# Mixture-of-experts layer: gate and up weights in chunks of 512 columns, gates and ups in turn, and weights kept stationary in all wide visits

## The chip, the cores and the metric

One core of one Trainium2 chip runs the whole layer. The metric is device time in microseconds, smaller is better. TensorE is called PE here (PEld is its weight load), VectorE is DVE, ScalarE is ACT, GpSimd is POOL, SyncE is SP.

## The reference, cut to what matters

The layer has two parts: attention over 1024 tokens of width 1024, and a mixture of 32 experts of which each token takes four. The change touches the experts alone:

```python
def expert_block(args):                  # a block of tokens and its expert
    xb, e = args
    gu = xb @ w_gate_up[e] + b_gate_up[e]          # 1024 -> 2048: 1024 gates, then 1024 ups
    gate = jnp.minimum(gu[:, :D_FF], SWIGLU_LIMIT)
    up = jnp.clip(gu[:, D_FF:], -SWIGLU_LIMIT, SWIGLU_LIMIT)
    glu = gate * jax.nn.sigmoid(SWIGLU_ALPHA * gate)
    return ((up + 1.0) * glu) @ w_down[e] + b_down[e]
```

All is float32. Each expert has 8 MB of gate and up weights and 4 MB of down weights, 403 MB for the 32.

## The kernel before, in words

Up to about 660 us the kernel does attention, its projections and the routing; then come the experts, then a final norm.

**Visits.** The experts are sorted by load and planned with fixed capacities (`PLAN`, 568 tokens down to 32). A visit is one expert with up to 512 tokens in blocks of up to 128; there are 33. Visits 0 to 10 have more than one block and form the stream "H"; visits 11 to 32 have one block and form the stream "L". Visits 7 to 10 hold 248, 208, 176 and 144 tokens, each in two blocks (128 and 120, 80, 48, 16). Visits 19 to 32 have at most 64 tokens and are called plain: their weights are used as they were loaded, in plain float32.

**Steps.** A visit has 16 gate-and-up steps, one for each of four column chunks `c` and four pairs of contraction rows `kh`, and 8 steps for the down weights. A step uses 256 x 512 weights. Two steps share one load of 1 MB (`weights`, L1170): for gates and ups this is two DMAs of 512 KB, 256 columns of gates and the 256 columns of ups that go with them, for down weights one DMA of 512 columns. In visits that aren't plain each step's weights are split in a high and a low part in fp32r (`cook`, L1296: ACT makes the high part, DVE and POOL together the low part, L1304), and a product is three matmuls: high by high, high by low, low by high.

**Two forms of matmul.** In the row form (L1526 to L1552) a block's tokens are the stationary operand and 512 columns of weights stream past: six matmuls of 512 columns a step for a block of over 64 tokens, four for one of at most 64 (its high and low parts sit side by side). The result has tokens on partitions, `glu` (L1434) works on it, and the product has to be turned on PE (`settle`, `turn`, L1365) before the down weights can use it. In the wide form (L1507 to L1525) 128 x 128 of the weights are stationary and all tokens of the visit stream past: 24 matmuls of `span` columns a step, into four PSUM banks, one for each 128 columns of gates or ups. The result stands with gate columns on partitions, `glu_w` (L1412) works on it, and nothing has to be turned. `span` (L74) is the number of tokens where that is at least 256, else 0 (row form): visits 0 to 6 use the wide form, visits 7 to 10 and all of L the row form. Down weights always use the row form.

**Order.** `merged` (L96) interleaves the steps of H and L so that loads and PE time stay in balance, by a cost for each step (`pe_cost`, L89) and one for what is loaded. The first 32 steps are of H alone. `places` (L126) gives every load and every split one of ten buffers and a time; a load is issued on SP's queue when the buffer's last reader is done. Each wide step costs 0.01 us a token in the planner's eyes, a row step 1.30 us for a full block.

Of the kernel before, what the change touches and what calls it, by code (L numbers as in the profile page):

```python
# [30 lines left out]
KP = 2  # L31
# [42 lines left out]
def span(v):  # L74

    n = sum(b[1] for b in v[2])
    return n if n >= 256 else 0
# [143 lines left out]
class Kernel:  # L221
# [948 lines left out]
    def weights(self, t, e, kind, c, kh):  # L1170

        nc = self.nc
        rows = slice(128 * KP * kh, 128 * KP * kh + 512)
        if kind == "g":
            for u in range(2):
                c0 = 1024 * u + 256 * c
                w = nc.sync.dma_start(t[:, :, 256 * u:256 * u + 256],
                                      self.w_gate_up[0][bass.ds(e, 1), rows, c0:c0 + 256]
                                      .rearrange("a (k p) n -> p (a k) n", p=128))
        else:  # L1180
            w = nc.sync.dma_start(t, self.w_down[0][bass.ds(e, 1), rows, 512 * c:512 * c + 512]
                                  .rearrange("a (k p) n -> p (a k) n", p=128))
        self.loaded = w.ins
# [60 lines left out]
    def experts(self):  # L1244
# [13 lines left out]
        xs, hs, accs = {}, {}, {}  # L1258
# [59 lines left out]
        def get_bias(n):  # L1318
# [14 lines left out]
            nt = max(nt for _, nt in vis[n][2])  # L1333
            o = groups(vis[n], nt)[-1]
            if st == "H":
                o, nt = 0, 128
# [75 lines left out]
        def glu_w(n, f, j, pg, pu):  # L1412

            sp = span(vis[n])
            if f == j == 0:
                hs[n] = parts("h", n)
            kk = 2 * f + j
            bc = biases[n]
            g = wp.tile([128, 512], F32, name="t", bufs=3)[:, :sp]
            a = wp.tile([128, 512], F32, name="sg", bufs=2)[:, :sp]  # L1420
            u = wp.tile([128, 512], F32, name="t", bufs=3)[:, :sp]
            V.tensor_scalar(g, pg[:, :sp], bc[:, kk:kk + 1], LIM, op0=ALU.add, op1=ALU.min)
            A.activation(a, g, AF.Sigmoid, scale=ALPHA)
            V.tensor_scalar(u, pu[:, :sp], bc[:, 8 + kk:9 + kk], LIM + 1.0, op0=ALU.add, op1=ALU.min)
            V.tensor_tensor(a, a, g, op=ALU.mult)
            V.scalar_tensor_tensor(a, u, 1.0 - LIM, a, op0=ALU.max, op1=ALU.mult)
# [7 lines left out]
        def glu(b, p, f):  # L1434
            nt = b["nt"]
            if len(late) == 4:
                settle(*late[0][1:3])
            t = wp.tile([128, 512], F32, name="t", bufs=3)[:nt]
            a = wp.tile([128, 256], F32, name="a", bufs=4)[:nt]
            bv = biases[b["n"]].rearrange("p (u n) -> p u n", u=2)[:, :, 256 * f:256 * f + 256]  # L1440
            t2 = t.rearrange("p (u n) -> p u n", u=2)
            *more, o = groups(vis[b["n"]], nt)
            V.tensor_tensor(t2, p[o:o + nt].rearrange("p (u n) -> p u n", u=2), bv[o:o + nt], op=ALU.add)
            for o in more:
                V.tensor_tensor(t, p[o:o + nt], t, op=ALU.add)
            V.tensor_scalar(t[:, 0:256], t[:, 0:256], LIM, None, op0=ALU.min)  # L1446
            V.tensor_scalar(t[:, 256:512], t[:, 256:512], LIM, -LIM, op0=ALU.min, op1=ALU.max)
            A.activation(a, t[:, 0:256], AF.Sigmoid, scale=ALPHA)  # L1448
            V.tensor_tensor(a, a, t[:, 0:256], op=ALU.mult)
            V.scalar_tensor_tensor(a, t[:, 256:512], 1.0, a, op0=ALU.add, op1=ALU.mult)  # L1450
            if f == b["j"] == 0:
                hs[b["n"]] = parts("h", b["n"])

            late.append((self.pe_time + 5.0, b, f, a))

        def settle(b=None, f=-1):

            for x in list(late):
                if x[0] <= self.pe_time or (x[1] is b and x[2] <= f):
                    late.remove(x)  # L1460
                    turn(x[3], hs[x[1]["n"]][1][x[1]["j"]][1:], x[1]["nt"], 2 * x[2])
# [32 lines left out]
        def mm(m):  # L1494
# [12 lines left out]
            if kind == "g" and span(vis[n]):  # L1507
# [4 lines left out]
                for j in range(2):  # L1512
                    for u in range(2):
                        ws = slice(256 * u + 128 * j, 256 * u + 128 * j + 128)
                        p = accs[n][2 * j + u][:, :sp]
                        for k in range(KP):
                            kk = KP * kh + k
                            mm(p, hi[:, k, ws], x[:, 0, kk, :], start=kk == 0, stop=False)  # L1518
                            mm(p, hi[:, k, ws], x[:, 1, kk, :], start=False, stop=False)  # L1519
                            mm(p, lo[:, k, ws], x[:, 0, kk, :], start=False, stop=kk == 7)  # L1520
                    if kh == NP - 1:
                        glu_w(n, c, j, accs[n][2 * j], accs[n][2 * j + 1])
# [3 lines left out]
            for b in blk[n]:  # L1526
                nt = b["nt"]
                if kind == "d":
                    settle(b, (KP * kh + KP - 1) // 2)
# [198 lines left out]
```

## Time and profile before

| | before |
|---|---|
| time, median of 3 runs | 2312.3 us (2306.0 to 2319.1) |
| the profiled execution | 2309.99 us, its span 2308.2 us |
| PE busy | 2110.6 us, 91% of the span |
| PE weight loads busy | 1516.9 us, 66% |
| DVE / ACT / POOL busy | 1635.7 / 964.0 / 1122.2 us |
| chain that ended last | PE 62%, DMA 14%, DVE 10%, issue 5%, POOL 4% |
| gate and up weights | 528 DMAs of 512 KB |
| down weights | 132 DMAs of 1024 KB |
| mean granted clock of TensorE | 0.97 |

Busy time of PE counts matmuls that overlap only once, so the page shows whether PE had something in flight, not how fast it went. How fast it goes is read from the starts of successive matmuls in the timeline. The chain is followed back from the last instruction; what it passes through is what the end waited for.

### The profile page before, as it was taken

What the parts mean: (1) busy time and instruction counts of PE and PEld (TensorE: products, weight loads), DVE (VectorE), ACT (ScalarE), POOL (GpSimd) and SP (SyncE); (2) the same over time, 40 slices, a digit from 0 to 9 for tenths busy, and PEclk for the clock granted to TensorE, in tenths of its full rate; (3) what the DMA queues carried; (4) which work ended last, traced back from release to release, by engine and by line L of the source; (5) the groups of instructions that cost most, each with busy time, mean ns of one, the idle gap of its engine ahead of it and who ended that gap; (6) DMA issues with size and microseconds to landing.
All of it is one profiled execution on the core that took longest, in us unless ns stands there. A gap on an engine that the chain in (4) does not pass through costs nothing.

```text
span 2308.2 us, 35345 instructions
## 1 busy us (share of the span) xinstructions
PE 2110.6 (91%) x11662; PEld 1516.9 (66%) x11662; DVE 1635.7 (71%) x3048; ACT 964.0 (42%) x1648; POOL 1122.2 (49%) x972
## 2 busy tenths in 40 slices
PE   4799998999878989889889999999999999999992
PEld 4787777777677877666555556655777686556551
DVE  7577645876576689789886545464777887767984
ACT  5343335763353455555553221122333343334443
POOL 1522222533565566897784233233455455455543
PEclk9899999999988999999999999999999999999996
DMA  7755486833567799999889999989998999899894
GB/s 250 181 156 160 140 224 170 193 78 131 133 173 191 231 284 296 290 275 295 257 278 338 351 290 337 335 298 318 286 294 269 312 310 321 281 309 299 300 315 158
DMA packets 468089, 583.40 MB, mean 253 GB/s; under 512 B 44245, under 2 KB 352645, under 8 KB 466057
## 3 DMA queue, kind: packets, MB, share of 16 engines
q1 hardware_dynamic: 444497, 528.41, 70.1%
q0 software_dynamic: 23408, 52.71, 11.2%
q8 instruction: 94, 1.54, 0.3%
q14 instruction: 90, 0.74, 0.1%
HBM read 522.41 MB, written 58.92 MB: 252 GB/s over the span
## 4 chain that ended last, share of the span: by engine, by line
PE 62%; DMA 14%; DVE 10%; issue 5%; POOL 4%; ACT 2%; SPq 1%; DVEq 0%; POOLq 0%; ACTq 0%
PE accL L1543 11%; DMA w<-in_w_gate_up 7%; PE accH L230 5%; PE accH L232 5%; PE accH L231 5%; PE accH L1518 4%; PE accH L1519 4%; PE accH L1520 4%; DVE w L1304 4%; POOL w L1304 3%; PE pm L230 3%; PE pm L232 3%; PE pm L231 2%; PE pt L1365 2%; PE poB L904 2%
## 5 line engine op out<-in xcount | busy, mean ns | idle before, releaser
L1304 POOL TENSOR_TENSOR w<-w,w 128x288 fp32r<-128x288 f32 x456 | 607.9, 1368 | 517.7 <-ACT w L1302 472.4
L1302 ACT ACTIVATE w<-w 128x1024 fp32r<-128x1024 f32 x456 | 469.6, 1053 | 502.7 <-DMA w<-in_w_gate_up 121.8
L1304 DVE TENSOR_TENSOR w<-w,w 128x736 fp32r<-128x736 f32 x456 | 499.0, 1103 | 183.4 <-ACT w L1302 172.2
L1518 PE MATMUL accH<-xH,w 128*128 128x256 f32 (+5 forms) x896 | 287.2, 323 | 3.3 <-ACT w L1302 1.5
L1519 PE MATMUL accH<-xH,w 128*128 128x256 f32 (+5 forms) x896 | 283.1, 316 | 0.4 <-DVE xH L238 0.4
L1520 PE MATMUL accH<-xH,w 128*128 128x256 f32 (+5 forms) x896 | 274.6, 317 | 0.6 <-POOL w L1304 0.5
L1518 PEld LDWEIGHTS accH<-xH,w 128*128 128x128 f32 x896 | 170.5, 191 | 47.6 <-issue 23.8
L1543 PE MATMUL accL<-w,xL 128*32 128x512 f32 (+3 forms) x896 | 181.3, 601 | 1.4 <-DVE y L1476 0.7
L1520 PEld LDWEIGHTS accH<-xH,w 128*128 128x128 f32 x896 | 171.1, 191 | 8.8 <-POOL w L1304 2.2
L1519 PEld LDWEIGHTS accH<-xH,w 128*128 128x128 f32 x896 | 171.2, 191 | 7.1 <-issue 1.6
L230 PE MATMUL accH<-w,hH 128*128 128x512 f32 (+3 forms) x368 | 151.4, 413 | 1.6 <-ACT w L1302 1.6
L231 PE MATMUL accH<-w,hH 128*128 128x512 f32 (+3 forms) x368 | 147.0, 399 | 0.0
L232 PE MATMUL accH<-w,hH 128*128 128x512 f32 (+3 forms) x368 | 144.7, 401 | 1.7 <-POOL w L1304 1.6
L1448 ACT ACTIVATE a<-t 32x256 f32<-32x256 f32 (+10 forms) x120 | 49.1, 412 | 175.7 <-DVE t L1446 175.2
L230 PE MATMUL accL<-w,xL 128*72 128x512 f32 (+4 forms) x256 | 104.7, 409 | 18.5 <-DVE y L1472 18.5
L232 PE MATMUL accL<-w,xL 128*72 128x512 f32 (+4 forms) x256 | 105.0, 411 | 14.7 <-POOL w L1304 13.9
L1478 POOL DMA_INDIRECT d_y<-y,lsH x54 | 88.6, 1640 | 46.5 <-DVE y L1472 33.5
L231 PE MATMUL accL<-w,xL 128*72 128x512 f32 (+4 forms) x256 | 103.9, 406 | 0.0
L1477 POOL TENSOR_TENSOR y<-y,gf 32x512 f32<-32x512 f32 (+6 forms) x40 | 63.9, 1598 | 70.7 <-DVE y L1476 70.6
L230 PEld LDWEIGHTS accH<-w,hH 128*128 128x128 f32 (+3 forms) x368 | 68.2, 186 | 45.8 <-issue 18.3
L230 PE MATMUL pm<-whi,hh 128*128 128x256 f32 x320 | 93.6, 293 | 2.1 <-ACT qs L538 1.0
L232 PE MATMUL pm<-wlo,hh 128*128 128x256 f32 x320 | 92.9, 291 | 0.0
(375 smaller groups left out, 4806.7 us busy)
## 6 DMA issues: line engine op xcount, KB each, us to landing
w<-in_w_gate_up SPq DMA_DIRECT2D x528, 512.0 KB
w<-in_w_down SPq DMA_DIRECT2D x132, 1024.0 KB
aw<-in_w_ada SPq DMA_DIRECT2D x64, 256.0 KB
wraw<-in_w_in SPq DMA_DIRECT2D x18, 512.0 KB
xt<-in_x SPq DMA_DIRECT2D x16, 512.0 KB
wa<-in_w_ada SPq DMA_DIRECT2D x8, 1024.0 KB
d_h<-zero SPq DMA_DIRECT2D x9, 512.0 KB
d_y<-zero SPq DMA_DIRECT2D x18, 256.0 KB
```

The lines of the kernel that those rows point to most:

```text
L230: mm(ps, lh, rh, start=start, stop=False)
L231: mm(ps, ll, rh, start=False, stop=False)
L232: return mm(ps, lh, rl, start=False, stop=stop).ins
L1302: A.activation(hi, w, AF.Copy)
L1304: eng.tensor_tensor(lo[:, :, cs], w[:, :, cs], hi[:, :, cs].bitcast(F32), op=ALU.subtract)
L1448: A.activation(a, t[:, 0:256], AF.Sigmoid, scale=ALPHA)
L1477: P.tensor_tensor(y, y, gf, op=ALU.mult)
L1478: s = P.indirect_dma_start(out=self.d_y[c], out_offset=bass.IndirectOffsetOnAxis(ap=b["ls"][:nt, 0:1], axis=0), in_=y, in_offset=None, com ...
L1518: mm(p, hi[:, k, ws], x[:, 0, kk, :], start=kk == 0, stop=False)
L1519: mm(p, hi[:, k, ws], x[:, 1, kk, :], start=False, stop=False)
L1520: mm(p, lo[:, k, ws], x[:, 0, kk, :], start=False, stop=kk == 7)
L1543: mm(p[o:o + nt], w[:, kk, :], hi[:, k, :], start=kk < len(at), stop=kk >= 8 - len(at))
```

## The change

Gate and up weights are loaded 512 columns at a time by one DMA of 1 MB: chunk 0 is the first half of the gates, chunk 1 the first half of the ups, then the second halves. Every visit with more than one block (0 to 10) uses the wide form for gates and ups. With at most 208 tokens (visits 8 to 10, "joined") the high and the low part of the tokens stream past the high weights in one matmul of twice the columns; the two halves of the sum are added behind it, with one more pass of ACT and one of DVE. A gate chunk leaves its activated gates in SBUF (`ga`, five buffers, or `a`, three) until the ups come. In the row form up to two pending products, of 512 columns each, wait to be turned, before it was four of 256. The planner's costs follow: 12 x KP x span / 2245 for a wide step, a formula of its own for joined visits. `mm` takes four groups of 128 columns of one kind in place of two groups of gates and ups:

```diff
 def span(v):
-    n = sum(b[1] for b in v[2])
-    return n if n >= 256 else 0
+    return sum(b[1] for b in v[2]) if len(v[2]) > 1 else 0
+def joined(v):
+    return 0 < span(v) <= 208
 def pe_cost(v, kind):
+    if kind == "g" and joined(v):
+        return 4 * KP * (2 * span(v) / 2245 + max(span(v) / 2245, 0.11))
     if kind == "g" and span(v):
-        return 12 * KP * span(v) / 2400
+        return 12 * KP * span(v) / 2245
...
         if kind == "g":
-            for u in range(2):
-                c0 = 1024 * u + 256 * c
-                w = nc.sync.dma_start(t[:, :, 256 * u:256 * u + 256],
-                                      self.w_gate_up[0][bass.ds(e, 1), rows, c0:c0 + 256]
-                                      .rearrange("a (k p) n -> p (a k) n", p=128))
+            c0 = 1024 * (c % 2) + 512 * (c // 2)
+            w = nc.sync.dma_start(t, self.w_gate_up[0][bass.ds(e, 1), rows, c0:c0 + 512]
+                                  .rearrange("a (k p) n -> p (a k) n", p=128))
...
+        def glu_w(n, c, j, p):
...
+            if joined(vis[n]):
+                A.activation(t, p[:, sp:2 * sp], AF.Copy)
+                V.scalar_tensor_tensor(t, p[:, :sp], bc, t, op0=ALU.add, op1=ALU.add)
+                V.tensor_scalar(t, t, top, None, op0=ALU.min)
+            else:
+                V.tensor_scalar(t, p[:, :sp], bc, top, op0=ALU.add, op1=ALU.min)
+            if c % 2 == 0:
+                a = gates[n, j] = wp.tile([128, WIDE], F32, name="ga", bufs=5)[:, :sp]
+                A.activation(a, t, AF.Sigmoid, scale=ALPHA)
+                V.tensor_tensor(a, a, t, op=ALU.mult)
+                return
...
+                for j in range(4):
+                    ws = slice(128 * j, 128 * j + 128)
+                    p = accs[n][j]
+                    for k in range(KP):
+                        kk = KP * kh + k
+                        if joined(vis[n]):
+                            mm(p[:, :2 * sp], hi[:, k, ws], x[:, :, kk, :], start=kk == 0, stop=False)
+                        else:
+                            mm(p[:, :sp], hi[:, k, ws], x[:, 0, kk, :], start=kk == 0, stop=False)
+                            mm(p[:, :sp], hi[:, k, ws], x[:, 1, kk, :], start=False, stop=False)
+                        mm(p[:, :sp], lo[:, k, ws], x[:, 0, kk, :], start=False, stop=kk == 7)
                     if kh == NP - 1:
-                        glu_w(n, c, j, accs[n][2 * j], accs[n][2 * j + 1])
+                        glu_w(n, c, j, p)
```

The row form's `glu` is divided in the same manner: each chunk adds the bias to 512 columns; a gate chunk then limits, activates and multiplies, an up chunk limits and multiplies into the kept gates.

## Rows read from the trace of the kernel before

**Rows 1.** Windows view, four stages of the experts; the header names the columns.

```profile
core 0: us, PE busy (x) PEld busy (x) DVE busy (x) ACT busy (x) POOL busy (x), PEclk, DMA share, GB/s
830.00:1245.00 415.00, 365.01 (x1655) 256.28 (x1653) 353.87 (x452) 223.27 (x290) 321.71 (x228) 0.97 0.92 284
1245.00:1940.00 695.00, 691.33 (x3756) 453.93 (x3753) 437.70 (x765) 203.24 (x306) 283.95 (x221) 1.00 0.97 312
1940.00:2262.00 322.00, 313.06 (x1471) 189.07 (x1470) 259.96 (x445) 129.46 (x186) 166.27 (x130) 0.99 0.89 293
2262.00:2308.00 46.00, 5.69 (x25) 3.42 (x23) 16.34 (x23) 14.33 (x28) 10.39 (x8) 0.61 0.61 197
```

**Rows 2.** Chain view of the first three of these stages, shares by line.

```profile
by line: DMA w<-in_w_gate_up 30.7%; POOL w L1304 13.6%; issue 10.7%; DVE w L1304 9.9%; DMA w<-in_w_down 6.2%; ACT w L1302 3.9%; PE accL L230 3.5%; PE accL L231 3.4%; PE accL L232 3.4%; DMA biasL<-in_b_gate_up 2.1%; SPq L1177 1.7%; DVE a L14
...
by line: PE accL L1543 29.4%; PE accH L1518 13.2%; PE accH L1519 11.9%; PE accH L1520 11.8%; PE accH L230 8.2%; PE accH L231 7.2%; PE accH L232 7.2%; PE pt L1365 4.2%; DMA w<-in_w_gate_up 1.6%; PE accH L1550 1.6%; PE accH L1549 1.4%; DMA d_
...
by line: PE accH L230 17.9%; PE accH L232 17.8%; PE accH L231 16.6%; PE accL L1543 12.0%; issue 6.9%; DMA w<-in_w_gate_up 5.3%; PE pt L1365 4.2%; PE accH L1550 3.4%; DVE w L1304 3.3%; PE accH L1549 3.0%; POOL w L1304 1.8%; ACT w L1302 1.3%;
```

**Rows 3.** Groups by line and shape, 1900 to 2285 us, PE: xcount, busy us, mean ns.

```profile
L230 PE MATMUL accH<-w,xH 128*128 128x512 f32 x128 | 54.1, 423 | 4.0 <-ACT w L1302 3.9
...
L1550 PE MATMUL accH<-w,xH 128*48 128x512 f32 x32 | 12.6, 408 | 0.0
...
L1365 PE MATMUL pt<-idt,a 128*128 128x128 f32 x32 | 6.3, 277 | 0.0
```

**Rows 4.** Timeline of PE, visit 7, row form; start us, us, what.

```profile
1945.85 0.50 PE L230 MATMUL accH<-w,xH 128*128 128x512 f32 x1
...
1951.62 0.64 PE L1543 MATMUL accL<-w,hL 128*32 128x512 f32 x4
```

**Rows 5.** Timeline of PE, wide form: visit 2 (456 tokens), then visit 6 (256).

```profile
1260.02 0.47 PE L1518 MATMUL accH<-xH,w 128*128 128x456 f32 x1
...
1265.21 1.07 PE L1543 MATMUL accL<-w,xL 128*56 128x512 f32 x4
...
1888.19 0.38 PE L1518 MATMUL accH<-xH,w 128*128 128x256 f32 x1
...
1894.06 1.06 PE L1543 MATMUL accL<-w,xL 128*32 128x512 f32 x6
```

**Rows 6.** Timeline of PE, visit 8: two turns between matmuls of the row form.

```profile
2065.34 0.38 PE L1365 MATMUL pt<-idt,a 128*128 128x128 f32 x2
2065.47 0.47 PE L230 MATMUL accH<-w,xH 128*80 128x512 f32 x1
```

**Rows 7.** DMA view, 1380 to 1388 us, then 2164 to 2172 us: packets, MB, share.

```profile
DMA packets 2902, 2.89 MB, mean 361 GB/s; under 512 B 80, under 2 KB 2902, under 8 KB 2902
...
q1 hardware_dynamic: 2902, 2.89, 105.0%
...
DMA packets 1425, 2.85 MB, mean 357 GB/s; under 512 B 32, under 2 KB 32, under 8 KB 1425
...
q1 hardware_dynamic: 1425, 2.85, 98.1%
```

**Rows 8.** DMA view, 830 to 1245 us.

```profile
DMA packets 92527, 117.81 MB, mean 284 GB/s; under 512 B 4883, under 2 KB 72040, under 8 KB 91800
```

**Rows 9.** Groups, DVE, 1900 to 2285 us (row form), then 1840 to 1910 (wide form).

```profile
L1443 DVE TENSOR_TENSOR t<-accH,biasH 128x512 f32<-128x512 f32 x16 | 11.0, 685 | 4.9 <-PE accH L232 4.8
...
L1450 DVE SCALAR_TENSOR_TENSOR a<-t,a 128x256 f32<-128x256 f32 x16 | 7.1, 441 | 0.1
...
L1426 DVE SCALAR_TENSOR_TENSOR sg<-t,sg 128x256 f32<-128x256 f32 x8 | 5.1, 634 | 0.1
...
L1422 DVE TENSOR_SCALAR t<-accH,biasC 128x256 f32<-128x256 f32 x8 | 3.8, 478 | 2.7 <-PE accH L1520 2.6
```

**Rows 10.** Page, costliest groups: fp32r weight loads and plain float32 matmuls; mean ns.

```profile
L1518 PEld LDWEIGHTS accH<-xH,w 128*128 128x128 f32 x896 | 170.5, 191 | 47.6 <-issue 23.8
L1543 PE MATMUL accL<-w,xL 128*32 128x512 f32 (+3 forms) x896 | 181.3, 601 | 1.4 <-DVE y L1476 0.7
```

More of the change, by code (lines that the diff above doesn't have):

```diff
@@ L1257, in experts @@
         regs, raw, cooked, lists, blk, biases, late = {}, {}, {}, {}, {}, {}, []
-        xs, hs, accs = {}, {}, {}
+        xs, hs, accs, gates = {}, {}, {}, {}
         self.pe_time = 0.0
@@ L1331, in get_bias @@
             bias = lp.tile([128, 2048], F32, name="bias" + st)
-            nt = max(nt for _, nt in vis[n][2])
+            nt = vis[n][2][0][1]
             o = groups(vis[n], nt)[-1]
-            if st == "H":
-                o, nt = 0, 128
             nc.sync.dma_start(bias[o:o + nt], self.b_gate_up[0][bass.ds(reg(n), 1), :].to_broadcast([nt, 2048]))
@@ L1410, in xform @@
             turn(b["xg"][:b["nt"]], xs[n][1][j][1:], b["nt"], 0, n == 0)
-        def glu_w(n, f, j, pg, pu):
+        def glu_w(n, c, j, p):
             sp = span(vis[n])
-            if f == j == 0:
-                hs[n] = parts("h", n)
[L1417 to L1426, printed above, removed]
+            kk = 4 * (c // 2) + j
+            bc = biases[n][:, 8 * (c % 2) + kk:8 * (c % 2) + kk + 1]
+            top = LIM + c % 2
+            t = wp.tile([128, 512], F32, name="t", bufs=3)[:, :sp]
+            if joined(vis[n]):
[9 more added lines that the diff above has]
+                return
+            if kk == 0:
+                hs[n] = parts("h", n)
+            a = gates.pop((n, j))
+            V.scalar_tensor_tensor(a, t, 1.0 - LIM, a, op0=ALU.max, op1=ALU.mult)
             w, blocks = hs[n]
@@ L1432, in glu_w, with glu @@
                 self.split(hi[:, kk, :], lo[:, kk, :], a[:, full:])
-        def glu(b, p, f):
+        def glu(b, p, c):
             nt = b["nt"]
-            if len(late) == 4:
-                settle(*late[0][1:3])
             t = wp.tile([128, 512], F32, name="t", bufs=3)[:nt]
-            a = wp.tile([128, 256], F32, name="a", bufs=4)[:nt]
-            bv = biases[b["n"]].rearrange("p (u n) -> p u n", u=2)[:, :, 256 * f:256 * f + 256]
-            t2 = t.rearrange("p (u n) -> p u n", u=2)
+            c0 = 1024 * (c % 2) + 512 * (c // 2)
+            bv = biases[b["n"]][:, c0:c0 + 512]
             *more, o = groups(vis[b["n"]], nt)
-            V.tensor_tensor(t2, p[o:o + nt].rearrange("p (u n) -> p u n", u=2), bv[o:o + nt], op=ALU.add)
+            V.tensor_tensor(t, p[o:o + nt], bv[o:o + nt], op=ALU.add)
             for o in more:
                 V.tensor_tensor(t, p[o:o + nt], t, op=ALU.add)
[L1446 to L1451, printed above, removed]
+            if c % 2 == 0:
+                if len(late) == 2:
+                    settle(*late[0][1:3])
+                a = b["a"] = lp.tile([128, 512], F32, name="a", bufs=3)[:nt]
+                V.tensor_scalar(t, t, LIM, None, op0=ALU.min)
+                A.activation(a, t, AF.Sigmoid, scale=ALPHA)
+                V.tensor_tensor(a, a, t, op=ALU.mult)
+                return
+            a = b.pop("a")
+            V.tensor_scalar(t, t, LIM, -LIM, op0=ALU.min, op1=ALU.max)
+            V.scalar_tensor_tensor(a, t, 1.0, a, op0=ALU.add, op1=ALU.mult)
+            if c == 1:
                 hs[b["n"]] = parts("h", b["n"])
-            late.append((self.pe_time + 5.0, b, f, a))
+            late.append((self.pe_time + 5.0, b, c // 2, a))
         def settle(b=None, f=-1):
@@ L1460, in settle @@
                     late.remove(x)
-                    turn(x[3], hs[x[1]["n"]][1][x[1]["j"]][1:], x[1]["nt"], 2 * x[2])
+                    turn(x[3], hs[x[1]["n"]][1][x[1]["j"]][1:], x[1]["nt"], 4 * x[2])
         def leave(b, p, c):
@@ L1528, in mm @@
                 if kind == "d":
-                    settle(b, (KP * kh + KP - 1) // 2)
+                    settle(b, (KP * kh + KP - 1) // 4)
                 if ("p", kind, c) not in b:
```

9 lines of the change are left out of this document (removed).

## The prediction

> **What bounds the kernel now.** I read the windows view first, over four stages of the experts [rows 1]. From 1245 to 1940 us PE has work in flight for 691 of 695 us at a granted clock of 1.00, and from 1940 to 2262 us for 313 of 322 us at 0.99. From 830 to 1245 us it has 365 of 415 us, at 0.97, while the DMA share is 0.92 and DVE and POOL are busy 85% and 78%. So there are two kinds of stage. The chain of each says what its end waits for [rows 2]: in the two later stages nearly every large share is PE, with gate and up loads at 1.6% and 5.3%; in the early one the loads of weights hold 30.7% and 6.2%, the splitting of weights (L1304, L1302) 27%, and PE's own lines about 10%. A change that shortens PE work pays after 1245 us; one that shortens loads pays before it. DMA is close behind PE in the middle, at a share of 0.97, and the last 46 us hold almost no PE work and are not touched.
>
> **PE in visits 7 to 10.** These run from about 1931 us on, in the PE-bound end. Their gates and ups are row-form matmuls: a block of over 64 tokens takes 96 of them a visit (16 steps of six), a smaller one 64. L230 has x128 for the four full blocks, 32 a visit, with L231 and L232 as often; the 48-token block has x32 on each of two lines [rows 3]. Four full blocks, the blocks of 120 and 80, and those of 48 and 16 make 384 + 192 + 128 = 704. In the timeline, 24 of them start between 1945.85 and 1951.62 us: 0.240 us each, 0.47 ns a column [rows 4]. That is 169 us.
>
> In the wide form 24 matmuls of 456 columns take 5.19 us and 48 of 256 take 5.87 us: 0.216 and 0.122 us each, again 0.47 to 0.48 ns a column, each with a weight load of its own [rows 5]. So the two forms stream columns at one rate, and only their number counts. Visit 7 after the change: 16 x 24 matmuls of 248 columns, 384 x 248 x 0.47 ns = 45 us (before 192 x 0.240 = 46; no gain). The joined visits have 128 matmuls each of 416, 352 and 288 columns on the high weights: 128 x 1056 x 0.47 ns = 64 us. Beside these are 128 each of 208, 176 and 144 columns on the low weights, and no row of this form is under 256 columns. Bounds: by columns alone 128 x 528 x 0.47 ns = 32 us; at the 0.122 us that 256 columns take, 47 us. I take 0.11 us each, 42 us, nearer to the row at 256, because a load of 128 columns of weights has to fit beneath each, and such a load is busy for 191 ns, only partly hidden [rows 10]. Sum 45 + 64 + 42 = 151 us, 18 us less than 169 (bounds 13 and 28).
>
> **Turns.** The wide form delivers the product already turned, so 64 transposes go (four visits, two blocks, eight each). Two of them take 0.13 us out of a run of matmuls [rows 6], which gives 64 x 0.065 = 4 us; by the busy time of a group of 32, 6.3 us [rows 3], it would be 13 us. I take 5, by the timeline, as PE doesn't wait for the whole length of one.
>
> **Loads.** The same bytes come in half the packets. Between 1380 and 1388 us almost all are of 1 KB: 1.05 x 16 x 8 us over 2902 packets is 46.3 ns each. Between 2164 and 2172 us nearly all are of 2 KB: 0.981 x 16 x 8 us over 1425 is 88.1 ns [rows 7]. Each pair of small packets that becomes one large saves 4.5 ns. From 830 to 1245 us there are 72040 - 4883 = 67157 packets of about 1 KB [rows 8]: 33600 x 4.5 ns over 16 engines is 9 us of DMA time. Weight loads hold 37% of that stage's chain, splits take turns with them at 27%, so I take 6 us, with bounds 0 and 18 (the saving counted twice, as the buffer also comes free sooner for the next load). In the PE-bound stages PE hides it: 528 DMAs of 512 KB are 135000 pairs of packets, 38 us in all, so some 29 us are left there to no effect. SP issues half as many of these DMAs, which nothing waits for beyond the 1.7% of the early chain.
>
> **What is added.** Joined visits read both halves of the sum: one ACT pass and one DVE pass more per group of 128 columns, 16 a visit. By rows, DVE in the row form spends on a block and chunk one PSUM pass of 0.685 us and five passes at about 0.44 us, 2.9 us, 23 us a visit; in the wide form 16 PSUM passes of 0.478 us and 24 others at no more than 0.634 us, again 23 us, at 256 columns, and the joined visits are narrower by a fifth to two fifths, which pays for their extra 16 passes [rows 9]. DVE stays at 81% of that stage [rows 1] and off the path. All four PSUM banks are now filled in these visits, and the next chunk's first matmul waits until the first bank is read: in joined visits by ACT and then DVE. The trace shows no such wait: 2 us, nearest to none, with bounds 0 (a step of L lies between) and 12 (both passes, 1 us [rows 9], at each of 12 chunk ends). In the row form of L four DVE instructions and one of ACT fewer are issued for each pair of chunks, off the path. The gates of L now wait for their ups before a turn; the four down steps on the first half of the products cover the last turn, and without them PE would wait about 2.4 us a visit, by one pass of 0.685 us and two of twice 0.44 [rows 9]. The order of steps moves too: with the new costs `merged` gives wide visits 0 to 6 more light steps beside them and starts visit 7 at position 638 of 792 instead of 616. That moves PE work, it adds none.
>
> **Sum.** -18 - 5 - 6 + 2 = -27 us. The profiled execution took 2310.0 us, its span 2308.2; it stands 2.3 us under the median of 2312.3. So 2283 us, 1.2 to 1.3% less. The forecast's own range is 2251 to 2305, with all bounds on one side. About 0.5%, 12 us, is what a measurement of this kernel can tell from no change.
>
> **Rivals.**
>
> *Loads become the bound in the middle.* The 22 light steps that move ahead of visit 7 bring 11 loads of 1 MB; at 312 GB/s [rows 1] that is 37 us of transfers put into a stage whose DMA share is 0.97. Against it: their PE time of some 11 us, the 3% of 695 us that is free, 21 us, and the saving in packets, two thirds of the 29 us above by the length of the stage, 19 us. 51 us against 37: it fits, if the loads come evenly. Where they don't, half to most of the gain is waited away, and the time is 2294 to 2312, say 2300. A joined visit whose splits come late would look the same.
>
> *Narrow fp32r matmuls run at a slower rate.* Every fp32r matmul of the expert stages streams at least 256 columns, so the rate below is open. The nearest other rate is that of plain float32: such a matmul of 512 columns lasts 0.60 us [rows 10], an fp32r one 0.42 [rows 3], about 0.37 ns a column more. At 0.84 ns a column visit 7 costs 384 x 248 x 0.84 = 80 us and the low-weight matmuls 57 us, together 50 us more than I have, and the time is 2333, slower than before. It decides at 256 columns: all 768 matmuls between 144 and 248 columns would show it. For it speaks only that no such row exists; against it, that the rate per column is the same at 256, 456 and 512.
>
> *Weight loads stop hiding.* After the change visits 7 to 10 have 1152 matmuls, each with its load, where there were 704: 448 more, and at 191 ns each [rows 10], unhidden, 86 us more, so 2369. The trace speaks against it: 48 matmuls of 256 columns with 48 loads pass in 0.122 us each [rows 5], less than a load lasts by itself. The Trainium skill (TensorE: Matmul & The Clock Gate, Part 3: Packing small matmuls) says that a weight load overlaps matmuls in flight only when it is for another group of rows, which all these 128-row loads are not; by its figure of 107 ns a load the extra ones would cost an estimated 48 us and turn the gain into a loss. The trace does not agree with it at 256 columns; no run here shows fewer.
>
> **How the numbers follow.** The forecast has 0.68: its largest term rests on a count and on one rate measured at three widths. The loads in the middle 0.15, the slow narrow rate 0.12, the unhidden loads 0.02, and 0.03 for something else, half of it slower. The range holds the forecast and the first rival, 0.83, so 2251 to 2312. Faster by over 0.5% is the forecast without its uppermost end, and the first rival's lowest, 0.67; within 0.5%, 0.17; slower, 0.16.
>
> **What would show it.** Right: in the timeline the low-weight matmuls of 144 to 208 columns and their neighbours start 0.10 to 0.12 us apart; the turns of accH products are gone; gate and up loads are 264 DMAs of 1 MB; PE stays at over 95% from 1300 us to the end; the early stage loses a few us. Wrong: matmuls of 248 columns that start 0.2 us apart, PE idle after 1300 us with splits waiting for loads, or PE waiting for DVE at the ends of chunks in visits 8 to 10.

## The result, and the profile after

The change takes 2288.4 us (median of 4 runs, 2281.1 to 2290.8) against 2311.0 us for the kernel before on the same chip: a ratio of 0.989, 95% interval 0.986 to 0.992. A second set of the same code gave 2292.1 against 2313.3 us, 0.990 (0.988 to 0.993). So 21 to 23 us are gained where 27 were forecast, and the time is inside the range.

The profiled execution of the change took 2281.1 us, its span 2279.3. It is the fastest of its runs; another profiled execution of the same code has a span of 2290.7 us. The kernel before shows the same spread, 2308.2 and 2298.8 us. Most of the difference lies ahead of visit 7, 11 of 11.4 us in the change and 7 of 9.4 in the kernel before. Stages are therefore compared by their own lengths, not by where they begin.

The page after the change: busy time, DMA packets and the loads of gate and up weights.

```profile
PE 2083.8 (91%) x12050; PEld 1551.4 (68%) x12050; DVE 1593.2 (70%) x2860; ACT 967.3 (42%) x1650; POOL 1112.3 (49%) x970
...
DMA packets 328243, 579.20 MB, mean 254 GB/s; under 512 B 40021, under 2 KB 78149, under 8 KB 326729
...
w<-in_w_gate_up SPq DMA_DIRECT2D x264, 1024.0 KB
```

The windows view after, over the stages that answer to [rows 1]: early, middle, visits 7 to 10, tail.

```profile
820.00:1235.00 415.00, 362.21 (x1629) 252.16 (x1628) 340.16 (x371) 220.24 (x257) 310.15 (x226) 0.97 0.88 288
1235.00:1935.00 700.00, 698.57 (x3872) 458.73 (x3870) 438.04 (x694) 203.58 (x292) 289.20 (x225) 1.00 0.94 321
1935.00:2243.00 308.00, 291.81 (x1811) 231.19 (x1807) 240.72 (x424) 139.76 (x243) 170.32 (x131) 0.96 0.79 265
2243.00:2279.00 36.00, 0.39 (x2) 0.00 (x0) 14.32 (x21) 13.64 (x27) 6.65 (x5) 0.57 0.72 244
```

The middle is still filled by PE to 99.8%, with DMA at 0.94 where it had 0.97. How long the early stage lasts can't be read here, as the windows were chosen; it is measured under e1. The third stage lost its fullness: PE has work in flight for 291.8 of 308 us, and its mean clock fell from 0.99 to 0.96. The tail is 36 us; before it was 40.5 us from the last expert matmul to the end.

The timeline of PE after, visit 7 (248 columns), then visit 8 (416 columns on the high weights, 208 on the low), the rows that answer to [rows 4, 5].

```profile
1937.17 0.28 PE L1534 MATMUL accH<-xH,w 128*128 128x248 f32 x1
...
1940.25 0.27 PE L1534 MATMUL accH<-xH,w 128*128 128x248 f32 x1
...
2028.15 0.37 PE L1532 MATMUL accH<-xH,w 128*128 128x416 f32 x1
2028.36 0.26 PE L1536 MATMUL accH<-xH,w 128*128 128x208 f32 x1
...
2030.55 0.37 PE L1532 MATMUL accH<-xH,w 128*128 128x416 f32 x1
```

Between the first two rows 27 matmuls start in 3.08 us, 0.114 us each: 0.46 ns a column, below 256 columns as above. Between the third and the last there are eight pairs in 2.40 us, 0.300 us a pair, of which the 416 columns take some 0.205 and the 208 the rest.

To see where the time went, I add, for every PE instruction from visit 7's first gate matmul to the last expert matmul, the time until the next one starts, by what it does. The last row is the stage just ahead, from the first matmul of the first visit with 56 tokens to visit 7. There are two executions of each kernel; "before again" is the run e7 below.

```
                                    before  before again  change  change again
gates and ups of visits 7 to 10      183.4     180.1       172.5      173.6
their turns                            8.4       8.6         0          0
down steps of visits 7 to 10          86.7      86.7        85.9       84.4
light visits' matmuls                 48.5      48.6        38.9       38.8
other turns                            9.2       9.5        10.3       10.8
the whole stretch                    336.6     333.8       308.4      308.5
after it, to the end                  40.5      41.1        35.9       36.1
56-token visit to visit 7            692.1     692.4       706.2      706.2
```

The stretch is 25 to 28 us shorter, but not all of that is gained. Of its 320 light matmuls 104 now stand ahead of visit 7. At the 0.152 us that each costs before, these are 16 us, while the row falls by only 10: the light matmuls that are left wait more. The stage ahead took in those 104, and from the early stage 44 wide matmuls of 456 columns, and is 14 us longer. The last three rows together are 1069.2 and 1067.3 us before, 1050.5 and 1050.8 after. So 17 to 19 of the 21 to 23 us are gained from the 56-token visit on. The other 2 to 6 us lie ahead of it, where two executions of the same code differ by some 8 us, and can't be placed.

### The profile page after: what moved, and what is told of

Read it like the earlier page. It is cut to its first block, busy times and chain, and to the rows that moved or that the text cites. A ratio compares the mean times of both kernels' runs of the same rounds, so it can differ in the third digit from the quotient of the medians.

```text
span 2279.3 us, 34822 instructions
## 1 busy us (share of the span) xinstructions
PE 2083.8 (91%) x12050; PEld 1551.4 (68%) x12050; DVE 1593.2 (70%) x2860; ACT 967.3 (42%) x1650; POOL 1112.3 (49%) x970
## 5 line engine op out<-in xcount | busy, mean ns | idle before, releaser
L1309 POOL TENSOR_TENSOR w<-w,w 128x288 fp32r<-128x288 f32 x456 | 595.2, 1364 | 544.3 <-ACT w L1307 518.9
L1309 DVE TENSOR_TENSOR w<-w,w 128x736 fp32r<-128x736 f32 x456 | 506.6, 1124 | 202.4 <-ACT w L1307 200.4
L1536 PE MATMUL accH<-xH,w 128*128 128x256 f32 (+9 forms) x1408 | 400.3, 296 | 2.7 <-POOL w L1309 1.8
L1534 PE MATMUL accH<-xH,w 128*128 128x256 f32 (+6 forms) x1024 | 322.0, 318 | 1.7 <-ACT xH L243 0.6
L1535 PE MATMUL accH<-xH,w 128*128 128x256 f32 (+6 forms) x1024 | 316.9, 311 | 0.3 <-DVE xH L244 0.3
L1536 PEld LDWEIGHTS accH<-xH,w 128*128 128x128 f32 x1408 | 272.1, 195 | 15.4 <-issue 5.0
L1534 PEld LDWEIGHTS accH<-xH,w 128*128 128x128 f32 x1024 | 194.5, 191 | 49.8 <-issue 27.3
L1535 PEld LDWEIGHTS accH<-xH,w 128*128 128x128 f32 x1024 | 195.4, 191 | 5.3 <-DVE xH L244 0.7
L1532 PE MATMUL accH<-xH,w 128*128 128x416 f32 (+2 forms) x384 | 116.2, 378 | 10.7 <-DVE t L1424 10.6
L1492 POOL DMA_INDIRECT d_y<-y,lsH x54 | 96.7, 1791 | 47.3 <-DVE y L1486 33.1
L1451 DVE TENSOR_TENSOR t<-accL,biasL 32x512 f32<-32x512 f32 (+8 forms) x88 | 60.5, 688 | 62.1 <-PE accL L1559 46.7
L1559 PEld LDWEIGHTS accL<-w,xL 128*32 128x32 f32 (+3 forms) x896 | 39.5, 115 | 84.0 <-issue 79.3
```

Of the source, the lines that this page charges most:

```text
L1309: eng.tensor_tensor(lo[:, :, cs], w[:, :, cs], hi[:, :, cs].bitcast(F32), op=ALU.subtract)
L1451: V.tensor_tensor(t, p[o:o + nt], bv[o:o + nt], op=ALU.add)
L1492: s = P.indirect_dma_start(out=self.d_y[c], out_offset=bass.IndirectOffsetOnAxis(ap=b["ls"][:nt, 0:1], axis=0), in_=y, in_offset=None, com ...
L1532: mm(p[:, :2 * sp], hi[:, k, ws], x[:, :, kk, :], start=kk == 0, stop=False)
L1534: mm(p[:, :sp], hi[:, k, ws], x[:, 0, kk, :], start=kk == 0, stop=False)
L1535: mm(p[:, :sp], hi[:, k, ws], x[:, 1, kk, :], start=False, stop=False)
```

## The experiments

**e5: the change again**, for its spread.

> The changed kernel itself, in the same session as the next ones, to compare with. 2288 us, within 4. Its profile also shows how much stages that no edit touches move from one execution to the next.

2292.1 us, as above. **e7: the kernel before again**, one run.

> The kernel before itself, a second profile. If the 40.5 us between the last matmul of the experts and the end are its own, they are there again and the change took about 5 us off the end; if that was chance, this shows about 36 us, as all kernels with the wide form in visits 7 to 10 do.

2300.6 us, span 2298.8. Gates and ups of visits 7 to 10 take 180.1 us here and their turns 8.6; the stretch after the last expert matmul is 41.1 us. The later stages repeat within 3 us, what lies before them moves by 7.

**e1: small packets.** The change with two DMAs for each load of gates and ups:

```diff
-            w = nc.sync.dma_start(t, self.w_gate_up[0][bass.ds(e, 1), rows, c0:c0 + 512]
-                                  .rearrange("a (k p) n -> p (a k) n", p=128))
+            for u in range(2):
+                cu = c0 + 256 * u
+                w = nc.sync.dma_start(t[:, :, 256 * u:256 * u + 256],
+                                      self.w_gate_up[0][bass.ds(e, 1), rows, cu:cu + 256]
+                                      .rearrange("a (k p) n -> p (a k) n", p=128))
```

> The changed kernel with each gate and up load of 512 columns issued again as two DMAs of 256 columns, so 528 DMAs of 512 KB in packets of 1 KB; all else as changed (2288 us). If larger packets are worth what I forecast for them, 6 us of the early stage, this takes about 2294 us. If the packets lie off the path everywhere, 2288 us, within 4. If loads would otherwise bind in the middle stage, where the changed order puts more of them, 2300 us or more, with PE waiting after 1300 us.

2293.8 us, ratio 0.993 (0.991 to 0.996), beside 2288.4 and 2292.1 for the change and 2290.7 for e6, which runs the change's instructions in the same order. By the time alone that is 2 to 5 us slower and just what was expected if the packets bring 6 us; but the intervals meet, so the time decides nothing. The stretch from the first expert matmul to the start of the 56-token visit takes 604.9 us with small packets, 601.0, 603.7 and 601.9 with large ones and the same order of steps, 605.6 and 598.0 in the kernel before. A gain of a few microseconds could hide in that; it isn't shown.

The waits view of the early stage, PE, shows that something else moved there. The first two rows are before (820 to 1245 us), the next two after (820 to 1235).

```profile
PE accL L230 <- DVE y L1472: 18.5, 6, 7.8
PE accL L232 <- POOL w L1304: 16.0, 15, 2.8
```

```profile
PE accL L238 <- POOL w L1309: 28.8, 15, 5.4
PE accL L238 <- DVE w L1309: 9.8, 7, 2.8
```

The columns are who waits for whom, total us, times, longest. DMA's share falls from 0.92 to 0.88, and PE now waits more for the splitting of weights. It is tempting to say that easier loads uncovered the splits. Two runs speak against it: e1, which has the change's order but small packets, and e4 below, which has large packets but the old order. Their rows (780 to 1240 us), e1 first:

```profile
PE accL L238 <- POOL w L1312: 18.1, 17, 3.5
PE accL L238 <- DVE w L1312: 10.4, 5, 3.3
```

```profile
PE accL L242 <- POOL w L1313: 15.9, 13, 4.5
...
PE accL L242 <- DVE w L1313: 2.3, 4, 0.7
```

These are single lines of the view. Summed over all lines of PE, in the 415 us that end at the start of the 56-token visit, the waits are:

```
                        before  again   change  again   e6     e1     e4
for POOL's splits        16.6    17.9    31.9    28.0   39.0   27.5   17.3
for DVE's splits          0.8     1.5    11.0    11.6    8.8   11.6    3.6
PE idle, all causes      50.0    46.3    52.8    50.4   55.9   48.7   44.2
```

So the waits for splits go with the order of steps, and not with the packets (one execution of e1 and of e4). And PE is idle for about as long in all of them: only the name of what it waits for changed.

**e2: the wide form alone.** The kernel before, with visits 7 to 10 in the wide form, three matmuls of their own width, and nothing else: same loads, same order of steps (for that the planner keeps its old costs, an edit not printed here).

```diff
-    n = sum(b[1] for b in v[2])
-    return n if n >= 256 else 0
+    return sum(b[1] for b in v[2]) if len(v[2]) > 1 else 0
```

> The kernel before with the wide form for visits 7 to 10 alone: 256-column halves of gates and ups, 1 KB packets and the order of steps as before; all four visits use three matmuls of the visit's own width (none joined). Theory A, narrow matmuls go by their columns at 0.47 ns: visits 8 to 10 need 95 us in place of 123, turns save 5, so about 2278 us. Theory B, each narrow matmul takes the 0.11 us that its load of weights needs: 127 us in place of 123, so about 2310 us. Theory C, narrow fp32r runs at the plain rate of 0.84 ns a column: over 2360 us.

2293.3 us, ratio 0.992 (0.990 to 0.995): most of the gain, but not for the forecast's reason. Matmuls of 144, 176 and 208 columns all start 0.112 us apart, so the gates and ups of the four visits take 180.3 us, no less than the 183.4 and 180.1 of the row form. The rate is theory B's, the time is not: it lies between the two. What goes is the turns (8.4 us) and 5 us of the end (35.3 us after the last matmul), while the light matmuls take 4 us more. Some 6 to 8 of the 19 us measured are not found in the profile.

**e3: not joined.** The change with three matmuls of their own width in visits 8 to 10 and without the extra passes.

```diff
-            if joined(vis[n]):
+            if False:
...
-                        if joined(vis[n]):
+                        if False:
```

> The changed kernel with joined visits computed as three matmuls of the visit's own width and without the extra passes of ACT and DVE; loads and order as changed. If the load of weights sets 0.11 us a matmul, PE needs 0.33 us a group of three where the joined pair needs 0.246 to 0.302: about 21 us more, less some 10 us of waits at chunk ends that go with the extra passes, about 2299 us. If narrow matmuls go by columns, PE needs 10 us less and the waits go too, about 2268 us.

2310.1 us, ratio 0.999 (0.997 to 1.001): slower than either theory's number. The timeline of PE, visit 10, 144 columns:

```profile
2195.76 0.28 PE L1534 MATMUL accH<-xH,w 128*128 128x144 f32 x1
...
2200.12 0.28 PE L1534 MATMUL accH<-xH,w 128*128 128x144 f32 x1
```

39 matmuls in 4.36 us are 0.112 us each, where 0.46 ns a column would give 0.066. Gates and ups take 184.8 us, 12 more than in the change, although the waits for DVE's first pass are down to 1.5 us. So joining is worth at least 12 us, by sparing a third of the matmuls of visits 8 to 10, in a run in which each would cost 0.112 us. The other 6 to 10 us are not found: this kernel's profiled execution (span 2298.8) was one of its fastest. Nor is it explained why it lies 17 us above e2, whose matmuls are the same.

**e4: the old order.** The change with the planner's costs of the kernel before, so that steps stand as they did.

```diff
-    cost = lambda p: pe_cost(vis[p[0]], p[1])
+    def cost(p):
+        v = vis[p[0]]
+        if p[1] == "g" and span(v) >= 256:
+            return 12 * KP * span(v) / 2400
+        return sum(block_cost(v, b[1]) for b in v[2]) + 0.12 * len(v[2])
```

> The changed kernel with the order of steps of the kernel before: the planner weighs steps by the old costs, all else as changed. If the moved order is neutral, 2288 us, within 4. If the waits at the chunk ends of joined visits come from having too few light steps between them, the old order, with 22 more light steps there, gives back about 10 us: 2278 us. If the moved order relieved the end more than it loaded the middle, this is slower, about 2296 us.

2286.6 us, 0.991 (0.988 to 0.994): the moved steps neither cost nor bring anything that shows. Here light steps stand beside visit 10, whose gates and ups take 36.2 us instead of 47.6; other waits take the room (PE waits 9.0 us once for a pass of the down steps, L1494).

This run shows one thing more. With the order of the kernel before, the stage from the 56-token visit to visit 7 takes 684.2 us, against 692.1 and 692.4 before and 693.5 in e2, though it holds 12 wide matmuls more. So the change makes this stage some 10 us quicker for the same work. The packets are not the reason: with small ones (e1) the stage takes 707.0 us beside the change's 706.2. PE idles 0.9 us here where it idled 2.6 to 3.6; what does the rest, the fewer passes and turns of the light visits or the chunks of the wide ones, no run separates.

**e6: product first.** In the last step of a joined chunk the products and their passes are written ahead of the next split.

```diff
+            late_cook = kind == "g" and kh == NP - 1 and joined(vis[n])
+            if late_cook:
+                mm(m)
             if m + LOOK < M:
                 cook(m + LOOK)
-            mm(m)
+            if not late_cook:
+                mm(m)
```

> The changed kernel, but at the last step of a chunk of a joined visit the matmuls and the passes that empty the PSUM banks are issued before the splitting of weights five steps ahead, not behind it. If the waits of PE at these chunk ends (10.6 us, and matmuls at half clock behind them) come from the passes standing behind splits in the queues of ACT and DVE, most of some 16 us goes: 2274 us. If they come from too little time between the chunks, or the bank's readers aren't queued behind splits, no change: 2288 us.

2290.7 us, 0.990 (0.988 to 0.993), no change, and PE's wait for L1424 is 10.6 us in four waits as in the change. This decides nothing: the instructions of every engine came out in the same order, as the edit changed only the order in which they are written. It is a third set of the change. The question was put again with e9.

**e9: six banks.** In the last joined visit, visit 10 (`last`), the products rotate through six PSUM banks, the two new ones those of the turns.

```diff
-                    accs[n] = [bank() for _ in range(4)]
+                    own = n != last
+                    accs[n] = [bank() if own or (4 * c + j) % 6 < 4 else
+                               scratch() for j in range(4)]
```

> The change with two more PSUM banks in turn for the last joined visit alone (144 tokens): its 16 products take six banks in rotation instead of four, the two new ones being those in which turns are made, which that late are nearly unused. The same matmuls, loads, splits and passes in the same order. Theory A (the next chunk waits because all banks of the last one still have to be read): of the change's 10.6 us of PE waiting for DVE's first pass (L1424), the 7.7 us that lie in this visit go, and with them most of the stretches at half clock behind them; visit 10's 128 matmul pairs from first to last take 37 to 41 us instead of 48.8, and the time is 2278 to 2283. Theory B (DVE and ACT have more to do in this visit than PE, so the splits would be late if the products were not): the wait moves to PE waiting for DVE's split (L1309), visit 10 stays at 47 to 50 us, and the time at 2288 to 2292.

First what happens in the change at a chunk's end: its timeline, all engines, visit 10.

```profile
2182.00 2.96 ACT L1307 ACTIVATE w<-w 128x1024 fp32r<-128x1024 f32 x3 [5.70 <-PE accH L1536]
...
2183.09 3.80 DVE L1309 TENSOR_TENSOR w<-w,w 128x736 fp32r<-128x736 f32 x3 [6.02 <-ACT w L1307]
...
2184.25 0.23 PE L1536 MATMUL accH<-xH,w 128*128 128x144 f32 x1
...
2184.98 0.66 ACT L1423 ACTIVATE t<-accH 128x144 f32<-128x144 f32 x3
...
2186.82 0.90 DVE L1424 SCALAR_TENSOR_TENSOR t<-accH,biasC,t 128x144 f32<-128x144 f32 x3
...
2187.23 0.61 PE L1532 MATMUL accH<-xH,w 128*128 128x288 f32 x1 [2.75 <-DVE t L1424]
...
2187.75 0.54 PE L1532 MATMUL accH<-xH,w 128*128 128x288 f32 x1
2188.09 0.32 PE L1536 MATMUL accH<-xH,w 128*128 128x144 f32 x1
2188.20 0.54 PE L1532 MATMUL accH<-xH,w 128*128 128x288 f32 x1
```

PE ends the chunk at 2184.5. ACT is in three splits until 2184.96 and only then empties banks; DVE is in its three splits until 2186.82 and then does its pass; PE starts again at 2187.2, and a pair then takes 0.45 us (2187.75 to 2188.20). Now the waits of PE from 1935 us on, in the change and, below it, with six banks.

```profile
PE accH L1532 <- DVE t L1424: 10.6, 4, 4.9
PE pt L1368 <- DVE biasC L1333: 2.6, 1, 2.6
```

```profile
PE accH L1538 <- DVE w L1309: 3.0, 4, 0.9
PE pt L1368 <- DVE biasC L1333: 2.8, 1, 2.8
PE accH L236 <- DVE t L1424: 2.2, 1, 2.2
...
PE accH L1534 <- DVE t L1424: 0.5, 1, 0.5
```

And the windows view by 4 us through visit 10: the change, then six banks (its visit begins 15 us later). Behind the stretch and its length stands PE's busy time, the third number from the end is the granted clock.

```profile
2180.00:2184.00 4.00, 4.00 (x35) 4.00 (x34) 0.91 (x1) 2.00 (x3) 3.09 (x3) 1.00 1.08 301
2184.00:2188.00 4.00, 1.25 (x7) 1.08 (x7) 3.97 (x7) 2.67 (x6) 4.00 (x4) 0.82 1.05 349
2188.00:2192.00 4.00, 4.00 (x19) 4.00 (x19) 3.06 (x11) 1.33 (x5) 0.30 (x1) 0.50 1.03 388
...
2208.00:2212.00 4.00, 0.03 (x1) 0.03 (x1) 3.97 (x6) 1.17 (x3) 3.84 (x4) 0.80 0.92 296
2212.00:2216.00 4.00, 4.00 (x17) 4.00 (x18) 3.75 (x10) 1.08 (x5) 1.49 (x2) 0.50 0.77 226
```

```profile
2200.00:2204.00 4.00, 4.00 (x35) 4.00 (x35) 4.00 (x7) 1.86 (x5) 3.19 (x3) 1.00 1.05 352
2204.00:2208.00 4.00, 4.00 (x35) 4.00 (x34) 3.97 (x15) 3.67 (x11) 1.22 (x2) 1.00 0.81 301
2208.00:2212.00 4.00, 4.00 (x35) 4.00 (x34) 4.00 (x7) 3.47 (x7) 3.27 (x4) 1.00 0.53 175
```

In visit 10 the change waits 2.75 and 4.9 us at chunk ends; with six banks neither wait is there, and behind chunk ends the clock stays at 1.00 where the change reads 0.50 (both have another such stretch at the visit's own start). A wait of 2.2 us for the same pass stands behind the visit's last chunk instead, before its first down step. The 0.5 us, and the 2.9 us of the change that it answers to, lie in visit 9, which the edit leaves alone. From its first gate matmul to its last visit 10 takes 37.5 us instead of 48.8 and 47.0 (its gates and ups alone 35.5 instead of 47.6 and 45.8), the gates and ups of all four visits take 163.6 instead of 172.5 and 173.6. Theory A holds; of theory B 3.0 us appear, as waits for splits. The time is 2284.6 us, 0.987 (0.985 to 0.990), a little above what A expected; it is 4 to 8 us under the three sets of the change, with intervals that overlap, so the gain is shown in the stage and only probable in the whole.

**e8: another cut of the splits.** The change, with DVE taking 384 of 512 columns of each split instead of 368, POOL the rest.

```diff
-            for eng, cs in ((V, slice(0, 368)), (P, slice(368, 512))):
+            for eng, cs in ((V, slice(0, 384)), (P, slice(384, 512))):
```

> The changed kernel with 384 of 512 columns of each split on DVE and 128 on POOL, before it was 368 and 144. If POOL's share of the splits is what PE waits for in the early stage (28.8 us of PE's waits there name it) and loads are not, POOL needs 0.15 us less a split and the time falls by 3 to 6 us, to 2283. If the loads set that stage, no change: 2288. If DVE, busy 82% there, takes POOL's place, it is slower, 2291.

2280.6 us, 0.986 (0.983 to 0.988): 8 to 12 us faster than the change, more than the 3 to 6 expected. The stretch from visit 0's first matmul of 256 columns to the start of the 56-token visit takes 577 us instead of 582 and 585, and 576 in e10, which has the same cut. So the gain lies in the early stage, but not plainly in the wait it was aimed at: PE's wait for POOL is 26.9 us against 28.8, and on this line executions of the change have 23.8 to 35.2. The wait for DVE is 4.8 against 9.8.

**e11: the same cut in the kernel before.**

> The kernel before with one number changed: splits cut at column 384 instead of 368, as in the run of the change with that cut (which was about 10 us faster than the change). If POOL's share of the splits holds the early stage whatever the loads' form, the time is 2300 to 2304, and the change's own gain is what stands between this and 2280.6, about 21 us as before. If POOL only became the bound because the change made loads quicker, nothing moves here: 2310 to 2314.

2312.0 us, 0.999 (0.997 to 1.001): nothing. The cut pays only with the change. The expectation's reason, quicker loads, isn't shown by this: the change also has another order of steps, and by e1 and e4 it is with the order that the waits for splits grew. The cut on the change in the old order, which would decide, wasn't run. PE's wait for POOL's splits in the early stage is 15.2 us here, and 16.0 in the kernel before.

**e10: six banks and the other cut.**

> Both edits on the change: six banks in the last joined visit, and the splits cut at column 384 instead of 368 (less for POOL). If the two gains come from different places (the cut in the early stage, the banks at the end) they add: by the cut alone 2280.6, and 8 to 12 us less with the banks, so 2269 to 2273. If the cut had also been what eased the end, the two overlap: 2276 to 2281.

2275.8 us, 0.985 (0.983 to 0.988), between the two expectations. The gates and ups of visits 7 to 10 take 157.3 us. This is the lowest median of all; against e8 alone (0.986) the difference isn't resolved.

## Why the prediction was right, point by point

**What bounds it: right, with one miss.** PE in the later stages is what paid, and the middle kept it busy. "The last 46 us ... are not touched" was wrong. The end of the timeline, DVE's last full blocks and POOL's last scatter, before and then after:

```profile
2264.73 0.75 DVE L1472 SCALAR_TENSOR_TENSOR y<-accH,lsH,gf 128x512 f32<-128x512 f32 x1 [2.99 <-PE accH L232]
2265.94 0.75 DVE L1472 SCALAR_TENSOR_TENSOR y<-accH,lsH,gf 128x512 f32<-128x512 f32 x1 [0.46 <-PE accH L232]
...
2278.99 1.35 POOL L1478 DMA_INDIRECT d_y<-y,lsL  x1 [0.97 <-DMA d_y<-y,lsH]
```

```profile
2235.77 0.75 DVE L1486 SCALAR_TENSOR_TENSOR y<-accH,lsH,gf 128x512 f32<-128x512 f32 x1 [3.01 <-PE accH L238]
...
2242.50 0.75 DVE L1486 SCALAR_TENSOR_TENSOR y<-accH,lsH,gf 128x512 f32<-128x512 f32 x1 [4.35 <-PE accH L238]
...
2250.60 1.35 POOL L1492 DMA_INDIRECT d_y<-y,lsL  x1 [1.49 <-DMA d_y<-y,lsH]
```

Before, the two halves of visit 10's output leave PE 1.2 us apart and their scatters queue up behind the last matmul; the last starts 11.3 us after it (2267.7). After, they leave 6.7 us apart, the first half's scatters are issued before the end, and the last scatter starts 7.2 us after the last matmul (2243.4). Every run in the row form at the end has 40 to 41 us behind the last expert matmul, every run in the wide form 35 to 37. Worth 5 us; that the earlier scatters are the reason is read from these rows.

**PE in visits 7 to 10: the mechanism right, the waits aside.** Forecast 169 to 151 us, 18 less. Measured 183.4 and 180.1 before and 163.6 us with the bank waits of visit 10 taken away (e9), 17 to 20 less; in the change itself only 4 to 11 less. Both forms take 11 to 14 us more than their steady rate, which cancels. By visit, forecast and change (and six banks): visit 7 45 and 46.6 (48.8), visit 8 39 and 40.2 (41.0), visit 9 35 and 38.1 (38.2), visit 10 31 and 47.6 (35.5). Visits 8 to 10 take 133.5 us in e2 with three matmuls each, and 114.7 in pairs with six banks. The 0.11 us for each low-weight matmul came out, as part of a pair: 0.300 us less 416 columns at 0.47 ns is 0.105. The reason given, that a load of weights has to fit beneath each, is borne out by the starts of loads (PEld) and matmuls, here in visit 10 of the change:

```profile
2181.69 0.23 PE L1536 MATMUL accH<-xH,w 128*128 128x144 f32 x1
2181.69 0.19 PEld L1532 LDWEIGHTS accH<-xH,w 128*128 128x128 f32 x1
2181.75 0.34 PE L1532 MATMUL accH<-xH,w 128*128 128x288 f32 x1
2181.80 0.19 PEld L1536 LDWEIGHTS accH<-xH,w 128*128 128x128 f32 x1
```

The matmul of 288 columns starts 0.06 us behind the one of 144, while the two loads are 0.11 us apart. At full clock no two loads of the wide form start less than 0.108 us apart, in the change or in e2. So the floor is of the loads and not of the single matmul, and a run of matmuls under 240 columns goes at 0.112 us each.

**Waits at chunk ends: the term that was mis-sized.** "2 us, nearest to none, with bounds 0 and 12". The waits are 10.6 us, at only 4 of the 12 chunk ends, but up to 4.9 us long, and matmuls at half clock follow them. In visit 10 both together are 10 to 12 us (47.6 and 45.8 against 35.5). The price of 1 us at a chunk end counted two passes; it did not count the splits queued ahead of them on ACT and DVE, 3 us and 3.8 us in the rows above. That the splits ahead are what makes the passes late is read from the timeline; e6 was meant to test it and didn't. The step of L that was to lie between chunks isn't there for visit 10, which has few light steps left; in e4, where they are there, it takes 36.2 us.

**A wait that has no term.** In the wide form a visit's biases are turned on PE too, and DVE empties the buffer. In the change this comes late before visit 10:

```profile
2169.41 1.06 PE L1559 MATMUL accL<-w,hL 128*32 128x512 f32 x8
...
2172.81 0.15 DVE L1333 TENSOR_SCALAR biasC<-pt 128x8 f32<-128x8 f32 x1
...
2173.10 0.61 PE L1368 MATMUL pt<-idt,a 32*128 32x32 f32 x4 [2.62 <-DVE biasC L1333]
```

PE waits 2.6 us (2.9 in the second execution, 2.8 with six banks), and the first matmuls of visit 10 run at half clock behind it. The kernel before has no such wait; e2, e3 and e4 use the wide form and don't have it either, so it hangs on when the copy comes up.

The Trainium skill (TensorE: Matmul & The Clock Gate, A second HAM failure mode: psum-queue depth-cycling) tells of a kernel whose matmul groups go round the PSUM banks: PE idles between the groups, and the clock falls and rises again. There it is frequent short idling; here it is single waits, of 2.75 and 4.9 us in visit 10. The trace agrees on the clock: 0.50 behind these in the change, 1.00 with six banks.

**Turns: right and small.** -5 forecast with a bound of 13; 8.4 us were there and are gone.

**Loads: not shown.** -6 forecast. Small packets (e1) are 2 to 5 us slower, within the noise, and the early stage is as long with either. The step that isn't borne out is the use of the chain: a stage whose chain holds loads at 37% needn't give back what loads save. PE idled there 46 to 50 us before and 50 to 56 us in the change.

**The moved order: right in the sum.** No price in the time (e4). But with it the waits for splits in the early stage grew, which the forecast didn't say.

**The stage ahead of visit 7: a gain without a term.** It does the same work some 10 us quicker (e4). The fewer passes of the light visits, which the forecast put "off the path", may be the reason; no run shows it.

**The sum.** -18 - 5 - 6 + 2 was forecast. Measured are -4 to -11 for the gates and ups with their waits, -8 for turns, -5 for the end, about +6 for light matmuls that wait more in visits 7 to 10, and in the stage ahead about -10 for quicker work but +10 for wide matmuls that came from the early stage. The loads are among the 2 to 6 us that can't be placed. That the total, 21 to 23 us, is near 27 is in part luck: the waits took back much of the largest term, and gains that the forecast put at nothing made up for some of it.

**Its signs.** The turns are gone and there are 264 DMAs of 1 MB. The other signs of being right are met in part or not: in visits 7 to 10 PE has work in flight for 94.7% of the time, just under the 95% named; the loss of the early stage is not resolved; low-weight matmuls and their neighbours start 0.07 to 0.10 and 0.18 to 0.21 us apart in turn, not 0.10 to 0.12. And one sign of being wrong came true: PE waits for DVE at the ends of chunks, in visits 9 and 10.

**The rivals.** *Loads bind in the middle*: no, PE has 698.6 of 700 us there. *Slow narrow rate*: no, 0.114 us at 248 columns and 0.112 at 144, where 0.84 ns a column would be 0.21 and 0.12. The second of these alone could not tell them apart; 144, 176 and 208 columns at the same 0.112 do. *Weight loads stop hiding*: as a sum no, as a floor of 0.108 us from load to load yes. The rule of the Trainium skill (TensorE: Matmul & The Clock Gate, Part 3: Packing small matmuls), that such a load overlaps only matmuls of other row groups, does not agree with 39 matmuls and their loads in 4.36 us.

## What to carry to other kernels

Loads of 128 x 128 weights have a floor, here 0.108 us from one to the next, so that matmuls with weights of their own went at 0.112 us or some 240 columns each: below that width, let two operands stream past the same weights in one matmul, and count loads, not columns. When a product now fills every PSUM bank, price the chunk's end by what is queued ahead of the first pass on the engines that empty the banks, not by the pass; a pair of spare banks was enough in the one visit where it was tried. When another name takes over in a view of waits, look whether the idle time as a whole moved, and which of the change's parts it goes with: here the packets looked like the reason, and two runs point to the order of steps. And try old settings again after a change: the cut of the splits, worth nothing before, gave 8 to 12 us afterwards.

## What was not expected of the hardware

Matmuls of 144, 176 and 208 columns with a weight load each all start 0.112 us apart, though the rate per column is 0.46 ns from 248 columns up; between two of them a load that is busy for 191 ns by itself is hidden. The loads show why: they start 0.11 us apart at the least, while a matmul of 144 columns can be followed by the next after 0.06 us. And a wait of PE costs more than its length: behind idle stretches of 2.75 and 4.9 us (up to 2187.2 and 2212.0) the granted clock reads 0.50 for the 4 us shown, one of its two levels (1.2 GHz), and a pair of 288 and 144 columns takes 0.45 us instead of 0.246 at full clock.
